# Second ConvFFN: seven products of quarters for 17 of its 22 pairs of up-projected tiles, their weight sums made beside the GLU

## The chip, the cores and the metric

The kernel runs on one core of a Trainium2 chip. Its time is the device time of one execution in microseconds (us), lower is better; the runs shown here are the median of three executions, 2302.68 us (2302.12 to 2303.56).

A core has TensorE (PE, matrix products into PSUM), VectorE (DVE), ScalarE (ACT), GpSimd (POOL) and SyncE (SP), each with a queue of instructions that it runs in order, and 16 DMA engines that all queues share. A DMA is issued by an instruction on SP's, ACT's or POOL's queue.

## The reference, cut to what matters

One step of a two-layer streaming encoder over T = 1088 tokens of width 1024 (1024 of a prompt, 64 of a sample). Layer 0 is windowed attention and a ConvFFN, layer 1 a state-space mixer that ends in a GLU (`y = (a + b_a) * sigmoid(b + b_b)`, where a and b are two products of the mixer's output with 1024 x 1024 weights) and a second ConvFFN. The change touches that GLU and the second ConvFFN:

```
u  = rms_norm(x, g6) @ w_up          # 1024 -> 2 x 2816: 22 gate tiles and 22 value tiles of 128 rows
u  = depthwise causal conv of width 3 over tokens (a bias and three taps per row)
gd = gelu(u[gate]) * u[value]        # 2816 rows
x  = x + rms_norm(gd @ w_down, g7)   # 2816 -> 1024
```

## The kernel before, in words

Rows of features lie on the 128 partitions, tokens along the free dimension. Tokens go in three blocks of 384, 384 and 320 (`BLK`). Every product of weights and activations is made of three passes over a high and a low part of both operands (`mm3`, L201 to L204: low activation, high activation, high activation by low weight), so that one 128 x 1024 weight tile against one block is 8 slices x 3 = 24 matmuls. ACT makes the high part of a weight tile and DVE the low part (L196, L197: `whl<-raw`); weight tiles are loaded in the order of a list (`wsrc`), two ahead of use, and six `big` buffers hold them.

**GLU** (L1204 to L1233). 24 tiles (8 rows of tiles x 3 blocks). Each has two PSUM tiles, `pb` and `pa`, of 24 matmuls; then ACT makes `sg` from `pb` (L1225) and DVE makes `y` from `pa` and `sg` (L1226). `sg` is one of five buffers (`t4`) that in the feed-forward hold the tiles `u` and `t`. `tile_` is a generator of two steps, the last 6 matmuls and the two instructions behind them being the second.

**Up-projection** (`up`, `up_start`, `up_block`, L359 to L392). For each of the 44 tiles: 3 blocks x 24 matmuls of a weight tile with the normalised input `h` (`hh`, `hl` in the trace), whose scale per token, `rb`, is multiplied in when DVE moves PSUM to `u` (L373, L375).

**Conv and gate** (`conv`, `gate`, L377 to L402). ACT makes the first tap (L381), DVE the other two (L382, L383), ACT the gelu (L396), DVE the product of gate and value in two pieces (L399, L401), which go to DRAM (`gd`) by SP's queue.

**Sums for the down-projection** (`sums_w`, `sums_g`, `sums`, L324 to L357). The down-projection of blocks 0 and 1 is done by seven products of quarters (`PRODUCTS`), which need sums of quarters of its weights (`jw`, written to `sd`) and of `gd` (`jg`, written to `td`). In the first ConvFFN the instructions are DVE's and the DMAs SP's (tiles `jt`); in the second both are POOL's (`E, Q`). Each of the 44 half-pairs has a turn (`aside`) in which one such job is started and the one before it is finished.

**What sets the order.** The program is written in this order, and a list scheduler with a priority per instruction (the order in which the program names them) lays each engine's queue; `order(x, y)` puts x behind y on the same engine.

Of the kernel before, what the change touches and what calls it, by code (L numbers as in the profile page):

```python
# [26 lines left out]
SIDE = 32  # L27

KCUT = (0, 12, 22)
GT = [[(4, "blkA")] * 3, [(4, "blkB"), (4, "blkB"), (2, "big")]]  # L30
# [11 lines left out]
class Core:  # L42
    def __init__(self, ctx, tc, a):
        self.ctx, self.tc, self.nc, self.a = ctx, tc, tc.nc, a
        nc = self.nc
        pool = lambda n, **k: ctx.enter_context(tc.tile_pool(name=n, bufs=1, **k))
        self.ready, self.wsrc = [], [("w_qk", 8), ("w_qk", 0), ("w_qk", 1), ("w_v", 0), ("w_v", 1)] + [("w_qk", m) for m in (2, 3, 9, 4, 5, 6, 7)]
        self.wsrc += [("w_o", m) for m in range(KD)]
        for i in range(2):
            self.wsrc += [("w_up", i, m + e) for m in range(KF) for e in (0, KF)]  # L50
            self.wsrc += [("w_part", i, k) + x[:3] for x in PRODUCTS for k in range(0, KH, 2)]
            self.wsrc += [("w_down", i, k, mh) for c in range(2) for mh in range(2) for k in range(KCUT[c], KCUT[c + 1], 2)]
            if i == 0:
# [113 lines left out]
    def load_unit(self, src):  # L167
        nc = self.nc
        raw = self.wts.tile([P, D], F32, name="raw", tag="raw", bufs=2)
        if src[0] == "w_part":  # L170
# [12 lines left out]
            nc.vector.tensor_sub(w[:, 1], raw, w[:, 0].bitcast(F32))  # L183
            return w
        ap = self.a[src[0]]
        if src[0] == "w_down":
# [4 lines left out]
        else:  # L191
            for i in src[1:]:
                ap = ap[i]
            self.loaded = nc.sync.dma_start(raw, ap)
        w = self.big([P, 2, D], "whl")
        nc.scalar.activation(w[:, 0], raw, AF.Copy)  # L196
# [112 lines left out]

    def ffn(self, i, h, rb, after, side=None, beside=lambda: None):  # L310

# [8 lines left out]


        E, Q = ((nc.vector, nc.sync), (nc.gpsimd, nc.gpsimd))[i]

        def sums_w(k):  # L324
            x = (jt[:, :2048] if i == 0 else js.tile([P, 2048], F32, name="jw")).rearrange("p (c h m) -> p c h m", c=2, h=2)
            Q.dma_start(x, a["w_down"][i, k::KH].rearrange("c p (h m) -> p c h m", h=2))
# [8 lines left out]
        def sums_g(k):  # L335
            x = jt[:, k % 2 * 1536:k % 2 * 1536 + 1536] if i == 0 else js.tile([P, 1536], F32, name="jg", bufs=2)
            x = x.rearrange("p (c b t) -> p c b t", c=2, b=2)
# [7 lines left out]
            Q.dma_start(td[:, k], x)  # L345

        jobs = {}

        def sums(j):

            for x in jobs.pop(j, []):
                next(x, None)
            k = (j // 2 - KH - 1, j // 2 - 2 * i)[j % 2]
            if 0 <= k < KH:
                x = (sums_g, sums_w)[j % 2](k)
                next(x)
                jobs[j + 1] = [x]  # L357

        def up_start(m):  # L359
            w = self.unit(("w_up", i, m))  # L360
# [4 lines left out]
            return w, u  # L365

        def up_block(w, u, b):
            t0, n = BLK[b]
            ps = self.mm_ps()
            for k in range(KD):  # L370
                self.mm3(ps[:, :n], w, slice(k * P, (k + 1) * P), h[b][0][:, k], h[b][1][:, k], k == 0, k == KD - 1)
            np_ = min(n, SEQ - t0)
            nc.vector.tensor_mul(u[:, t0 + 2:t0 + 2 + np_], rb[:, t0:t0 + np_], ps[:, :np_])  # L373
            if np_ < n:
                nc.vector.tensor_mul(u[:, SEQ + 4:], rb[:, SEQ:], ps[:, np_:n])  # L375

        def conv(m, u):  # L377
# [4 lines left out]
            nc.vector.scalar_tensor_tensor(t, u[:, 1:T + 3], cw(1, m), t, op0=ALU.mult, op1=ALU.add)  # L382
            nc.vector.scalar_tensor_tensor(t, u[:, 2:T + 4], cw(2, m), t, op0=ALU.mult, op1=ALU.add)  # L383
            return t
# [9 lines left out]
        def gate(f, us):  # L394
# [3 lines left out]
            tb = conv(KF + f, us.pop(KF + f) if KF + f in us else up([KF + f])[KF + f])  # L398
            nc.vector.tensor_mul(ta[:, :SEQ], ta[:, :SEQ], tb[:, :SEQ])  # L399
            nc.sync.dma_start(gd[:, f, :SEQ], ta[:, :SEQ])  # L400
            nc.vector.tensor_mul(ta[:, SEQ + 2:], ta[:, SEQ + 2:], tb[:, SEQ + 2:])  # L401
            nc.sync.dma_start(gd[:, f, SEQ:], ta[:, SEQ + 2:])  # L402

        turns = iter(range(2 * KF))

        def aside():
# [5 lines left out]
            sums(j - 1)  # L412

        us = up([0, KF, 1])
        gate(0, us)
        if i == 0:
            jt = self.yp.tile([P, 3072], F32, name="jt", tag="ypA", bufs=2)
        else:
            js_ctx = tc.tile_pool(name="js", bufs=1)
            js = js_ctx.__enter__()  # L420
        aside()
        for f in range(1, KF):
            if f == KF - 2:
                us = up([f, KF + f, f + 1])
# [4 lines left out]
        if i == 1:  # L429
            js_ctx.__exit__(None, None, None)  # L430
        nc.gpsimd.dma_start(a["o_conv"][i], cst.rearrange("p m s j -> p (m s j)"))
# [8 lines left out]
        def operand(p):  # L440
# [625 lines left out]
    def ssm(self, after):  # L1066
# [234 lines left out]
def build(tc, a):  # L1301
    nc = tc.nc
    with ExitStack() as ctx:
# [27 lines left out]
        def then(post, xs, xo, pre):  # L1331
# [61 lines left out]
```

## Time and profile before

| | |
|---|---|
| median of three runs | 2302.68 us |
| the profiled execution, its own time | 2296.63 us |
| its span | 2294.8 us |
| mean granted TensorE clock over the span | 0.986 |
| busy in the span: PE, DVE, ACT, POOL | 97%, 67%, 42%, 20% |
| GLU, its matmuls | 1315 to 1513 us |
| second up-projection, its matmuls | 1513 to 2039 us |
| second down-projection and the end | 2039 to 2295 us |

The profile is of one execution that took 6 us less than the median. An engine's busy time is the time in which an instruction of it runs. A matmul of 384 columns is shown as 0.33 to 0.35 us long but the next starts 0.17 us after it, since they overlap: the pace of PE is read from starts. "A <- B" in the columns on idle time and waits means that A's instruction began when B's had ended.

### The profile page before, as it was taken

To read this page: it belongs to the slowest core of one execution; us is meant where nothing else is said; L and a number is where in the kernel's file an instruction comes from. 1 tells how busy PE (TensorE), PEld (TensorE's weight loads), DVE (VectorE), ACT (ScalarE), POOL (GpSimd) and SP (SyncE) were. 2 spreads that over 40 slices of the span, in tenths; PEclk is the share of its full clock that TensorE was granted. 3 is DMA by queue.
4 is the path that set the end of the run, shared out by engine and by line. 5 is a ranking of instruction groups with operands and counts; after the bars stand their busy time and mean duration, and the time that the engine had idled before them with its cause. 6 is when DMAs were issued, how large, how long until landed. Compare 5 with 4: busy or idle time off the path is not lost.

```text
span 2294.8 us, 35768 instructions
## 1 busy us (share of the span) xinstructions
PE 2217.1 (97%) x13995; PEld 2149.1 (94%) x13995; DVE 1545.3 (67%) x2740; ACT 955.5 (42%) x1743; POOL 462.4 (20%) x416
## 2 busy tenths in 40 slices
PE   8999999999999999999978899999999999999997
PEld 7987799999999999999966699999999999999997
DVE  8677648989877786767757821397665555466764
ACT  5256756422343332555545631353222222245543
POOL 5222005100224223001100000154442132221000
PEclk9999999999999999999988999999999999999999
DMA  5100015655345655877759731155553333358773
GB/s 193 36 27 22 19 61 180 230 194 199 113 135 182 200 174 175 280 269 237 241 189 301 230 99 37 37 180 193 183 211 129 120 135 134 135 176 297 227 255 100
DMA packets 191001, 374.98 MB, mean 163 GB/s; under 512 B 23952, under 2 KB 114864, under 8 KB 187888
## 3 DMA queue, kind: packets, MB, share of 16 engines
q1 hardware_dynamic: 172736, 320.99, 42.1%
q0 software_dynamic: 9776, 47.21, 5.8%
q10 hardware_dynamic: 8320, 4.49, 0.9%
q8 instruction: 110, 1.80, 0.3%
q14 instruction: 59, 0.48, 0.1%
HBM read 262.10 MB, written 110.54 MB: 162 GB/s over the span
## 4 chain that ended last, share of the span: by engine, by line
PE 50%; DVE 6%; DMA 6%; ACT 3%; issue 2%; POOL 1%; SPq 1%; ACTq 0%; DVEq 0%; POOLq 0%
PE mm L202 14%; PE mm L204 14%; PE mm L203 14%; DMA raw<-sd 1%; PE pb L202 1%; PE pb L204 1%; PE pb L203 1%; PE pa L202 1%; PE pa L203 1%; PE pa L204 1%; DMA raw<-in_w_down 1%; DMA yd<-ys 1%; DMA prm<-b 1%; DMA prm<-oc 1%; DVE whl L197 1%
## 5 line engine op out<-in xcount | busy, mean ns | idle before, releaser
L202 PE MATMUL mm<-hl,whl 128*128 128x384 f32 (+1 forms) x2232 | 736.4, 330 | 11.0 <-ACT whl L196 7.4
L204 PE MATMUL mm<-hh,whl 128*128 128x384 f32 (+1 forms) x2232 | 734.3, 329 | 1.9 <-DVE whl L197 1.9
L203 PE MATMUL mm<-hh,whl 128*128 128x384 f32 (+1 forms) x2232 | 735.8, 330 | 0.0
L202 PEld LDWEIGHTS mm<-hl,whl 128*128 128x128 f32 x2232 | 420.8, 189 | 12.7 <-ACT whl L196 7.4
L204 PEld LDWEIGHTS mm<-hh,whl 128*128 128x128 f32 x2232 | 420.8, 189 | 2.7 <-DVE whl L197 2.7
L203 PEld LDWEIGHTS mm<-hh,whl 128*128 128x128 f32 x2232 | 421.1, 189 | 0.1
L196 ACT ACTIVATE whl<-raw 128x1024 fp32r<-128x1024 f32 x168 | 176.8, 1057 | 415.1 <-PE mm L204 330.2
L202 PE MATMUL mm<-gt,whl 128*128 128x384 f32 (+1 forms) x968 | 317.9, 329 | 2.3 <-ACT whl L196 1.8
L204 PE MATMUL mm<-gt,whl 128*128 128x384 f32 (+1 forms) x968 | 316.7, 328 | 0.7 <-DVE whl L197 0.7
L203 PE MATMUL mm<-gt,whl 128*128 128x384 f32 (+1 forms) x968 | 316.8, 328 | 0.0
L197 DVE TENSOR_TENSOR whl<-raw,whl 128x1024 fp32r<-128x1024 f32 x168 | 216.1, 1290 | 95.9 <-ACT whl L196 95.7
L373 DVE TENSOR_TENSOR u<-rb,mm 128x384 f32<-128x384 f32 (+1 forms) x264 | 131.7, 506 | 184.5 <-PE mm L204 184.3
L202 PEld LDWEIGHTS mm<-gt,whl 128*128 128x128 f32 x968 | 182.5, 189 | 3.2 <-ACT whl L196 2.0
L204 PEld LDWEIGHTS mm<-gt,whl 128*128 128x128 f32 x968 | 182.4, 189 | 1.0 <-DVE whl L197 1.0
L203 PEld LDWEIGHTS mm<-gt,whl 128*128 128x128 f32 x968 | 182.5, 189 | 0.0
L182 ACT ACTIVATE whl<-raw 128x1024 fp32r<-128x1024 f32 x84 | 82.8, 986 | 154.9 <-PE mm L204 60.9
L183 DVE TENSOR_TENSOR whl<-raw,whl 128x1024 fp32r<-128x1024 f32 x84 | 95.7, 1144 | 75.2 <-ACT whl L182 74.4
L383 DVE SCALAR_TENSOR_TENSOR t<-u,ppt,t 128x1090 f32<-128x1090 f32 x88 | 137.8, 1565 | 1.5
L382 DVE SCALAR_TENSOR_TENSOR t<-u,ppt,t 128x1090 f32<-128x1090 f32 x88 | 131.3, 1492 | 9.8 <-ACT t L381 7.4
L301 POOL TENSOR_TENSOR y<-y,xl 128x768 f32<-128x768 f32 (+1 forms) x16 | 30.3, 1892 | 491.5 <-DVE y L298 397.8
L381 ACT ACTIVATE t<-u,ppt 128x1090 f32<-128x1090 f32 x88 | 114.3, 1299 | 12.9 <-DVE t L383 6.8
L396 ACT ACTIVATE t<-t 128x1090 f32<-128x1090 f32 x44 | 49.1, 1117 | 132.7 <-DVE t L383 132.5
(345 smaller groups left out, 3690.0 us busy)
## 6 DMA issues: line engine op xcount, KB each, us to landing
raw<-in_w_up SPq DMA_DIRECT2D x88, 512.0 KB, 3.9
raw<-in_w_down SPq DMA_DIRECT2D x74, 512.0 KB, 4.4
gd<-t SPq DMA_DIRECT2D x44, 512.0 KB, 3.0
raw<-sd SPq DMA_DIRECT2D x40, 512.0 KB, 4.5
pm<-prm SPq DMA_DIRECT2D x32, 522.0 KB, 7.1
gr<-td SPq DMA_DIRECT2D x40, 384.0 KB, 6.1
jt<-in_w_down SPq DMA_DIRECT2D x11, 1024.0 KB, 5.8
sd<-jt SPq DMA_DIRECT2D x11, 1024.0 KB, 4.0
```

Of the source, the lines that this page charges most:

```text
L182: nc.scalar.activation(w[:, 0], raw, AF.Copy)
L183: nc.vector.tensor_sub(w[:, 1], raw, w[:, 0].bitcast(F32))
L196: nc.scalar.activation(w[:, 0], raw, AF.Copy)
L197: nc.vector.tensor_sub(w[:, 1], raw, w[:, 0].bitcast(F32))
L202: nc.tensor.matmul(out, w[:, 0, sl], xl, start=start, stop=False)
L203: nc.tensor.matmul(out, w[:, 0, sl], xh, start=False, stop=False)
L204: self.last_mm = nc.tensor.matmul(out, w[:, 1, sl], xh, start=False, stop=stop)
L373: nc.vector.tensor_mul(u[:, t0 + 2:t0 + 2 + np_], rb[:, t0:t0 + np_], ps[:, :np_])
L381: nc.scalar.activation(t, u[:, 0:T + 2], AF.Identity, bias=cb(m), scale=cw(0, m))
L382: nc.vector.scalar_tensor_tensor(t, u[:, 1:T + 3], cw(1, m), t, op0=ALU.mult, op1=ALU.add)
L383: nc.vector.scalar_tensor_tensor(t, u[:, 2:T + 4], cw(2, m), t, op0=ALU.mult, op1=ALU.add)
L396: nc.scalar.activation(ta, ta, AF.Gelu_apprx_tanh)
```

## The change

In the second ConvFFN the pairs f = 5 to 21 (`PLAIN = 5`) make their two tiles for blocks 0 and 1 by seven products of quarters (`seven`): the quarters are gate and value row tiles (two), the halves of the 1024 input rows (two), and blocks 0 and 1 (two). Each product is 4 slices x 3 passes = 12 matmuls of 384 columns. Block 2 is computed as before.

What goes with it:

- Sums of the weights' quarters (`su` in DRAM; two halves for each of 17 pairs, 34 jobs) are made in the GLU: `sums(f, e)` there loads two pieces of 256 KB on POOL's queue into a `t4` tile `sj`, makes four DVE operations of 128 x 256, and stores 512 KB on POOL's queue. `beside()` starts one after each of the GLU's 48 half steps until all are started, and finishes the one of two half steps before.
- In the ConvFFN each of the 17 pairs loads two weight units more (`w_sum`, 512 KB, split on ACT and DVE as the others are).
- The seven products need the normalised activations and sums of them. `ys`, the residual stream's tiles that the norm left in SBUF, are multiplied in place with scale and gain on DVE (`normed`: 16 operations of 128 x 384 at f = 2, 8 of 128 x 320 at f = 4), summed (`input_sums`: 8 of 128 x 768 at f = 3), and split into high and low parts on ACT and DVE over `h`'s own tiles and two of `yp` (`into_place`: six of 128 x 1536 at f = 4, one at f = 3, two of 128 x 1280 at f = 5). `rb` is then in the operands, not in the move from PSUM.
- For a pair by seven products DVE moves PSUM to `u` by seven additions of 128 x 384 (one product goes by ACT's copy, one stays in PSUM for an addition); block 2 is moved by ACT from the pair f = 6 on.
- `sums_w` and `sums_g` of the second ConvFFN are DVE's, with DMAs on POOL's queue, and `sums_w` starts six pairs later. `gd` of the second ConvFFN is stored by POOL's queue. Gate times value is one operation over 1090 columns, in both ConvFFNs. The tiles that pair 20 of the second ConvFFN took ahead (`up([f, KF + f, f + 1])`) are left to the first.

The core of the diff:

```diff
+PLAIN = 5
@@ the list of weight units
-            self.wsrc += [("w_up", i, m + e) for m in range(KF) for e in (0, KF)]
+            for m in range(KF):
+                sums = [("w_sum", m, e) for e in range(2)] if i == 1 and m >= PLAIN else []
+                self.wsrc += [("w_up", i, m)] + sums + [("w_up", i, m + KF)]
@@ ffn
-        E, Q = ((nc.vector, nc.sync), (nc.gpsimd, nc.gpsimd))[i]
+        E, Q = nc.vector, (nc.sync, nc.gpsimd)[i]
...
+            if normed:
+                nc.scalar.activation(u[:, t0 + 2:t0 + 2 + np_], ps[:, :np_], AF.Copy)
+                nc.scalar.activation(u[:, SEQ + 4:], ps[:, np_:n], AF.Copy)
+                return
...
-            nc.vector.tensor_mul(ta[:, :SEQ], ta[:, :SEQ], tb[:, :SEQ])
-            nc.sync.dma_start(gd[:, f, :SEQ], ta[:, :SEQ])
-            nc.vector.tensor_mul(ta[:, SEQ + 2:], ta[:, SEQ + 2:], tb[:, SEQ + 2:])
-            nc.sync.dma_start(gd[:, f, SEQ:], ta[:, SEQ + 2:])
+            nc.vector.tensor_mul(ta, ta, tb)
+            Q.dma_start(gd[:, f, :SEQ], ta[:, :SEQ])
+            Q.dma_start(gd[:, f, SEQ:], ta[:, SEQ + 2:])
...
+        def input_sums():
+            b11, b21, b12, b22 = (half(x[b], j) for b in range(2) for j in range(2))
+            t1, t4 = (self.big([P, 4, 384], "t", F32) for _ in range(2))
+            t2 = ts.tile([P, 4, 384], F32, name="t2", tag="t2")
+            for o, u, v in ((t1, b12, b11), (b12, b22, b12), (t2, b22, t1), (t4, b21, t2)):
+                for k in (slice(0, 2), slice(2, 4)):
+                    self.order(V.tensor_sub(o[:, k], u[:, k], v[:, k]), self.last_conv)
...
+        def seven(f, first):
...
+            nc.scalar.activation(g1, product(w, 0, "b11"), AF.Copy)
+            V.tensor_add(g0, g1, product(w, 1, "b21"))
+            ws = self.unit(("w_sum", f, 0))
+            V.tensor_add(g1, g1, product(ws, 0, "t2", True))
+            p3 = product(ws, 1, "b22", True)
+            if not first:
+                up_block(w, ug, 2, True)
+            ws = self.unit(("w_sum", f, 1))
+            V.tensor_add(v1, g1, product(ws, 0, "t3", True))
+            V.tensor_add(g1, g1, p3)
+            p5 = product(ws, 1, "t1", True)
+            V.tensor_add(g1, g1, p5)
+            w = self.unit(("w_up", i, KF + f))
+            V.tensor_add(v0, v1, product(w, 1, "t4"))
+            V.tensor_add(v1, v1, p5)
+            up_block(w, uv, 2, not first)
...
         for f in range(1, KF):
-            if f == KF - 2:
+            if i == 1 and f == 2:
+                normed((0, 1))
+            if i == 1 and f == 3:
+                late = input_sums()
+            if i == 1 and f == PLAIN - 1:
+                us = up([f, KF + f])
+                into_place(*late)
+                normed((2,))
+            if i == 1 and f >= PLAIN:
+                us = seven(f, f == PLAIN)
...
@@ ssm, the GLU
+        def sums(f, e):
+            x = self.t4([P, 2, 2, 256], "sj")
+            for j in range(2):
+                nc.gpsimd.dma_start(x[:, j], a["w_up"][1, j * KF + f].rearrange("p (c q) -> p c q", c=2)[:, :, 256 * e:256 * e + 256])
+            yield
...
+            V.tensor_add(a22, a21, a22)
+            V.tensor_sub(a21, a11, a21)
+            V.tensor_sub(a11, a22, a11)
+            V.tensor_sub(a12, a12, a11)
+            nc.gpsimd.dma_start(su[f, e], x.rearrange("p j c q -> p j (c q)"))
...
             for x in order[:3] * 2 + [x for x in order[3:] for _ in range(2)]:
                 next(x)
+                beside()
```

Three places of the queues show what moves. The first is DVE's queue in the pairs 2 to 4 of the second ConvFFN, before the change: only conv, gate, PSUM moves and weight splits stand there.

```order
L382 SCALAR_TENSOR_TENSOR t<-u,ppt,t 128x1090
L373 TENSOR_TENSOR u<-rb,mm 128x256
L375 TENSOR_TENSOR u<-rb,mm 128x64
L197 TENSOR_TENSOR whl<-raw,whl 128x1024
L383 SCALAR_TENSOR_TENSOR t<-u,ppt,t 128x1090
L399 TENSOR_TENSOR t<-t 128x1024
```

After the change (L402 is the second conv tap, L392 and L394 the PSUM moves, L418 the gate product, L208 the weight split; L456 are the sums of the input, L438 the splits):

```order
L402 SCALAR_TENSOR_TENSOR t<-u,ppt,t 128x1090
L456 TENSOR_TENSOR t<-y 128x768 x2
L418 TENSOR_TENSOR t<-t 128x1090
L456 TENSOR_TENSOR y<-y 128x768
L456 TENSOR_TENSOR t_15202<-y,t 128x768
L392 TENSOR_TENSOR u<-rb,mm 128x256
L394 TENSOR_TENSOR u<-rb,mm 128x64
L456 TENSOR_TENSOR y<-y 128x768
L456 TENSOR_TENSOR t_15202<-y,t 128x768
L438 TENSOR_TENSOR t_15212<-t,t_15211 128x1536
L456 TENSOR_TENSOR t<-y,t_15202 128x768
L374 MEMSET u 128x2
```

Right behind these rows stand the last PSUM move of block 0 and the weight splits of pair 4: the eight sums and the first split have moved ahead of them.

The second place is the same queue in a pair by seven products at which both kinds of sums for the down-projection run (f from 12 to 16; L489 to L502 are the additions out of PSUM, L339 to L342 the sums of `jw`, L351 to L354 those of `jg`):

```order
L342 TENSOR_TENSOR jw<-jw 128x512
L353 TENSOR_TENSOR jg<-jg 128x384
L491 TENSOR_TENSOR u<-u,mm 128x384
L418 TENSOR_TENSOR t<-t 128x1090
L208 TENSOR_TENSOR whl<-raw,whl 128x1024
L354 TENSOR_TENSOR jg<-jg 128x384
L208 TENSOR_TENSOR whl<-raw,whl 128x1024
L496 TENSOR_TENSOR u<-u,mm 128x384
L497 TENSOR_TENSOR u<-u,mm 128x384
L499 TENSOR_TENSOR u<-u,mm 128x384
L501 TENSOR_TENSOR u<-u,mm 128x384
```

In the program before, the operations on `jw` and `jg` stand on POOL's queue, each job between its own load and store, as here for `jw`:

```order
L326 DMA jw<-in_w_down 128x2x1024
L329 TENSOR_TENSOR jw<-jw 128x512
L330 TENSOR_TENSOR jw<-jw 128x512
L331 TENSOR_TENSOR jw<-jw 128x512
L332 TENSOR_TENSOR jw<-jw 128x512
L333 DMA sd_14364<-jw 128x2048
```

A pair's share of DVE's queue has grown by these eight sums, two weight splits (four instead of two) and one addition out of PSUM, less the moves of block 2, which ACT has now.

The third place is POOL's queue at the GLU. Before, the store of the mixer's state is followed at once by the norm behind the GLU:

```order
L1204 DMA out_o_st<-fo 128x128
L301 TENSOR_TENSOR y<-y,xl 128x768
L273 TENSOR_SCALAR gx<-y,ppt 128x384
L301 TENSOR_TENSOR y<-y,xl 128x768
L274 TENSOR_TENSOR hl<-gx,hh 128x384
```

After, 102 DMAs stand between the two (`L312` is the norm's addition now). They begin so:

```order
L1310 DMA out_o_st<-fo 128x128
L1319 DMA sj<-in_w_up 128x2x256 x6
L1327 DMA su<-sj 128x1024 x2
L1319 DMA sj<-in_w_up 128x2x256 x2
L1327 DMA su<-sj 128x1024
```

They end so:

```order
L1319 DMA sj<-in_w_up 128x2x256 x4
L1327 DMA su<-sj 128x1024
L1319 DMA sj<-in_w_up 128x2x256 x2
L1327 DMA su<-sj 128x1024 x3
L312 TENSOR_TENSOR y<-y,xl 128x768
```

Each store (L1327) waits for DVE's four sums, and the loads behind it in the queue start only once it is issued.

## Rows read from the trace of the kernel before

**Rows 1.** The profile page, part 1: busy us of each engine, share, instructions.

```profile
PE 2217.1 (97%) x13995; PEld 2149.1 (94%) x13995; DVE 1545.3 (67%) x2740; ACT 955.5 (42%) x1743; POOL 462.4 (20%) x416
```

**Rows 2.** Busy us by stretch: PE, PEld, DVE, ACT, POOL, clock, DMA share, GB/s.

```profile
1340.00:1476.00 136.00, 136.00 (x814) 136.00 (x814) 30.67 (x50) 34.91 (x51) 0.00 (x0) 1.00 0.13 39
1560.00:1608.00 48.00, 48.00 (x293) 48.00 (x292) 41.69 (x53) 19.93 (x28) 22.92 (x16) 1.00 0.54 196
1608.00:2039.00 431.00, 431.00 (x2616) 431.00 (x2615) 241.64 (x328) 109.47 (x165) 124.07 (x103) 1.00 0.41 145
...
440.00:600.00 160.00, 159.86 (x966) 159.86 (x967) 144.76 (x421) 47.01 (x69) 0.00 (x0) 1.00 0.51 181
```

**Rows 3.** Waits of PE, 1512 to 2039 us: us in total, times, longest.

```profile
PE mm L202 <- POOL hl L274: 0.4, 1, 0.4
```

**Rows 4.** Timeline of PE in the second up-projection: start us, duration us.

```profile
1799.69 0.31 PE L204 MATMUL mm<-hh,whl 128*128 128x320 f32 x1
...
1801.59 0.34 PE L202 MATMUL mm<-hl,whl 128*128 128x384 f32 x1
...
1802.13 0.34 PE L202 MATMUL mm<-hl,whl 128*128 128x384 f32 x1
...
1804.22 0.33 PE L202 MATMUL mm<-hl,whl 128*128 128x384 f32 x1
```

**Rows 5.** DVE by line and shape, first up-projection, 400 to 570 us.

```profile
L382 DVE SCALAR_TENSOR_TENSOR t<-u,ppt,t 128x1090 f32<-128x1090 f32 x15 | 20.3, 1351 | 0.2
...
L197 DVE TENSOR_TENSOR whl<-raw,whl 128x1024 fp32r<-128x1024 f32 x15 | 18.2, 1220 | 1.0 <-ACT whl L196 1.0
L373 DVE TENSOR_TENSOR u<-rb,mm 128x384 f32<-128x384 f32 x27 | 14.4, 550 | 0.4 <-PE mm L204 0.4
...
L330 DVE TENSOR_TENSOR jt<-jt 128x512 f32<-128x512 f32 x10 | 7.0, 697 | 0.0
```

**Rows 6.** DVE by line and shape, second up-projection, 1560 to 2039 us.

```profile
L383 DVE SCALAR_TENSOR_TENSOR t<-u,ppt,t 128x1090 f32<-128x1090 f32 x42 | 67.6, 1608 | 1.3
...
L438 DVE TENSOR_TENSOR gt<-gr,gt 128x768 fp32r<-128x768 f32 x4 | 3.6, 954 | 0.1
```

**Rows 7.** Second conv tap, 1560 to 2039 us: duration ns min/median/max, first and last start.

```profile
L383 DVE SCALAR_TENSOR_TENSOR t<-u,ppt,t x42: 1348/1356/2382, 1564.5 to 2030.8; 128x1090 f32<-128x1090 f32 x42
```

**Rows 8.** ACT by line and shape, second up-projection, 1560 to 2039 us.

```profile
L381 ACT ACTIVATE t<-u,ppt 128x1090 f32<-128x1090 f32 x43 | 55.8, 1298 | 8.8 <-DVE t L383 6.8 <-DMA gd<-t 2.0
L196 ACT ACTIVATE whl<-raw 128x1024 fp32r<-128x1024 f32 x35 | 37.1, 1060 | 228.9 <-PE mm L204 228.9
L396 ACT ACTIVATE t<-t 128x1090 f32<-128x1090 f32 x21 | 23.5, 1118 | 59.8 <-DVE t L383 59.8
```

**Rows 9.** GLU, 1340 to 1513 us, by line and shape.

```profile
L1226 DVE SCALAR_TENSOR_TENSOR y<-pa,ppt,sg 128x384 f32<-128x384 f32 x16 | 9.8, 616 | 69.4 <-ACT sg L1225 69.4
```

**Rows 10.** POOL's DMA issues, 1512 to 2039 us: busy us, mean ns.

```profile
L326 POOL DMA_DIRECT2D jw<-in_w_down x11 | 7.8, 711 | 45.7 <-DMA sd<-jw 43.3 <-PE mm L204 2.4
...
L333 POOL DMA_DIRECT2D sd<-jw x11 | 6.3, 577 | 3.3 <-POOL jw L332 3.3
```

**Rows 11.** DMA issues, 1512 to 2039 us: KB each, median us to landing.

```profile
jw<-in_w_down POOLq DMA_DIRECT2D x11, 1024.0 KB, 5.7
sd<-jw POOLq DMA_DIRECT2D x11, 1024.0 KB, 4.4
gd<-t SPq DMA_DIRECT2D x21, 512.0 KB, 2.7
...
raw<-in_w_down SPq DMA_DIRECT2D x1, 256.0 KB, 2.5
```

**Rows 12.** Busy us by stretch behind a wait of PE in the first up-projection.

```profile
782.10:785.50 3.40, 3.40 (x12) 3.40 (x11) 2.25 (x3) 1.60 (x4) 3.32 (x2) 0.51 0.95 311
785.50:790.00 4.50, 4.50 (x27) 4.50 (x27) 2.46 (x3) 0.00 (x0) 4.36 (x4) 1.00 0.47 135
```

**Rows 13.** Waits of PE, 570 to 930 us: us in total, times, longest.

```profile
PE wps L948 <- DVE kt L942: 9.1, 4, 3.4
```

More of the change, by code (lines that the diff above doesn't have):

```diff
@@ L306, in post_norm, with ffn @@
         return apply
-    def ffn(self, i, h, rb, after, side=None, beside=lambda: None):
+    def ffn(self, i, h, rb, after, side=None, beside=lambda: None, x=None, g=None):
         nc, tc, a = self.nc, self.tc, self.a
@@ L345, in sums_g @@
             Q.dma_start(td[:, k], x)
+        w0 = (PLAIN + 1) * i
+        starts = {2 * (k + w0) + 1: sums_w(k) for k in range(KH)}
+        starts.update({2 * (k + KH) + 2: sums_g(k) for k in range(KH)})
         jobs = {}
@@ L412, in aside, with half, split, normed @@
             sums(j - 1)
+        def half(v, j):
+            return v[:, 4 * j:4 * j + 4]
+        def split(hi, lo, src):
+            nc.scalar.activation(hi, src, AF.Copy)
+            nc.vector.tensor_sub(lo, src, hi.bitcast(F32))
+        def normed(bs):
+            for b in bs:
+                t0, n = BLK[b]
+                for k in range(KD):
+                    v = nc.vector.scalar_tensor_tensor(x[b][:, k], x[b][:, k], g[:, k:k + 1], rb[:, t0:t0 + n], op0=ALU.mult, op1=ALU.mult)
+                    self.order(v, self.last_conv)
@@ new lines, in input_sums @@
+        def input_sums():
+            V = nc.vector
+            b11, b21, b12, b22 = (half(x[b], j) for b in range(2) for j in range(2))
[4 more added lines that the diff above has]
+                    self.order(V.tensor_sub(o[:, k], u[:, k], v[:, k]), self.last_conv)
+            op["t1"] = [ts.tile([P, 4, 384], F32R, name=f"t1{j}") for j in range(2)]
+            split(*op["t1"], t1)
+            return t2, t4
@@ new lines, in into_place @@
+        def into_place(t2, t4):
+            todo = [("b11", 0, 0), ("b21", 0, 1), ("t2", t2), ("b22", 1, 1), ("t3", 1, 0), ("t4", t4)]
+            for name, src, *j in todo:
+                if j:
+                    hi, lo = (half(v, j[0]) for v in h[src][:2])
+                    src = half(x[src], j[0])
+                else:
+                    y = self.yp.tile([P, 2, 4, 384], F32R, name="th", tag="ypA", bufs=2)
+                    hi, lo = y[:, 0], y[:, 1]
+                op[name] = hi, lo
+                split(hi, lo, src)
@@ new lines, in seven, with product @@
+        def seven(f, first):
+            V = nc.vector
+            ug, uv = u_tile(f), u_tile(KF + f)
+            g0, g1, v0, v1 = (u[:, 2 + 384 * j:386 + 384 * j] for u in (ug, uv) for j in range(2))
+            def product(w, j, o, sums=False):
+                ps = self.mm_ps()[:, :384]
+                for k in range(4):
+                    c = (k // 2 * 4 + 2 * j + k % 2 if sums else 4 * j + k) * P
+                    self.mm3(ps, w, slice(c, c + P), op[o][0][:, k], op[o][1][:, k], k == 0, k == 3)
+                return ps
+            w = self.unit(("w_up", i, f))
+            if first:
+                up_block(w, ug, 2)
+            nc.scalar.activation(g1, product(w, 0, "b11"), AF.Copy)
[14 more added lines that the diff above has]
+            up_block(w, uv, 2, not first)
+            return {f: ug, KF + f: uv}
@@ L418, in ffn @@
         else:
-            js_ctx = tc.tile_pool(name="js", bufs=1)
-            js = js_ctx.__enter__()
+            ts_ctx = tc.tile_pool(name="ts", bufs=1)
+            ts = ts_ctx.__enter__()
+            op = {}
         aside()
         for f in range(1, KF):
-            if f == KF - 2:
+            if i == 1 and f == 2:
[8 more added lines that the diff above has]
+                us = seven(f, f == PLAIN)
+                if f == PLAIN:
+                    for j in range(2):
+                        split(half(h[2][0], j), half(h[2][1], j), half(x[2], j))
+            if i == 0 and f == KF - 2:
                 us = up([f, KF + f, f + 1])
@@ L1206, in ssm, with beside @@
         ws = {}
+        su = self.su = self.dram.tile([KF, 2, P, 2, 512], F32, name="su")
+        def sums(f, e):
+            x = self.t4([P, 2, 2, 256], "sj")
+            for j in range(2):
+                nc.gpsimd.dma_start(x[:, j], a["w_up"][1, j * KF + f].rearrange("p (c q) -> p c q", c=2)[:, :, 256 * e:256 * e + 256])
+            yield
+            a11, a12, a21, a22 = x[:, 0, 0], x[:, 0, 1], x[:, 1, 0], x[:, 1, 1]
+            V = nc.vector
+            V.tensor_add(a22, a21, a22)
[3 more added lines that the diff above has]
+            nc.gpsimd.dma_start(su[f, e], x.rearrange("p j c q -> p j (c q)"))
+        jobs = iter([sums(f, e) for f in range(PLAIN, KF) for e in range(2)])
+        loaded = []
+        def beside():
+            loaded.append(next(jobs, iter(())))
+            next(loaded[-1], None)
+            if len(loaded) > 2:
+                next(loaded.pop(0), None)
         with self.boundary():
```

42 lines of the change are left out of this document (24 added, 18 removed).

## The prediction

> **What bounds the kernel now.** I read the page first: PE is busy 97% of the span and no other engine over 67% [rows 1]. Then the stretches: in the second up-projection PE is busy for 431.00 of 431 us, in the GLU for 136.00 of 136, both at a granted clock of 1.00, which is the higher level, 2.4 GHz [rows 2]. The view of waits finds 0.4 us of PE waiting for any engine from 1512 to 2039 us [rows 3]. So both places run at PE's own pace; a matmul less there is time less, and work added to another engine costs something only where PE comes to wait for it. The timeline gives the pace: 12 starts of 384 columns in 1804.22 − 1802.13 = 2.09 us, 0.174 us each; 13 of 320 columns in 1.90 us, 0.146 us each [rows 4]. A pair of tiles is 96 × 0.174 + 48 × 0.146 = 23.7 us now. Of that DVE is busy 241.64 / 431 = 56%, so 13.3 us, and ACT 25% [rows 2].
>
> **What goes.** A pair of quarter products has 7 × 12 = 84 matmuls of 384 columns instead of 96. In 17 pairs that is 204 matmuls fewer, 204 × 0.174 = **35.5 us**, and a pair of 84 × 0.174 + 7.0 = 21.6 us. The whole term is on the path, because nothing else ends a wait there. The pace of the new matmuls is taken as that of the old: operands of the same 128 x 128 and 128 x 384 form, weights still changed for each.
>
> The Trainium skill (TensorE: Matmul & The Clock Gate, section Back-to-back issue gap) gives the isolated gap of a matmul at the full clock as columns / 2.4 GHz plus 2.5 ns, an estimate of 162.5 ns for 384 columns. By it the term would be 33.2 us; the trace's 174 ns is longer and decides.
>
> **What DVE gets in a pair by seven products.** Durations come from the first up-projection, where DVE makes the same sums and POOL is idle [rows 2, 5]:
> - four weight splits of 1.22 us, 4.9 (two before);
> - four conv operations of 1.35, 5.4;
> - the gate product over 1090 columns, at most a conv's 1.35, taken as 1.3;
> - seven additions out of PSUM, as the multiplication out of PSUM of 0.55, 3.9.
>
> That is 15.5 us. The sums moved from POOL add 4 × 0.70 = 2.8 (pairs 6 to 16) and, as 384 columns from SBUF are taken at the same 0.55, 4 × 0.55 = 2.2 (pairs 12 to 21): 18.3, 20.5 and 17.7 us against PE's 21.6. In the five pairs 12 to 16 DVE is at 95%. What a DVE that full costs PE, the first up-projection shows: 144.76 of 160 us busy, 90%, and PE loses 0.14 us [rows 2]. A relief goes the other way: with POOL summing, the second conv tap takes 1608 ns on average and up to 2382, while its median is 1356 [rows 6, 7]; the 88 POOL operations leave, so the undisturbed durations are right for after. I take 0. Below nothing it can't go, since PE has no idle time to give back there; above, if every operation took 10% more, 22.5 us in the five pairs, 0.9 × 5 = 4.6. ACT gets four splits of 1.06, two taps of 1.30, a gelu of 1.12 [rows 8], a copy of 384 columns and two moves of block 2 (together at most three taps, 3.9): 11.9 us at most of 21.6, so it hides.
>
> **The hand-over, pairs 2 to 5.** DVE gets, once: 16 scalings at the GLU's 0.62 [rows 9], 9.9; eight sums of 768 at 0.95 [rows 6], 7.6; seven splits of 1536, which by the slope from 384 (0.55) to 768 (0.95) are 0.95 + 2 × 0.40 = 1.76, 12.3; eight scalings of 320 at about 0.55, 4.4; two splits of 1280 at about 1.5, 3.0. In all 37 us, in four pairs in which DVE has 4 × (23.7 − 13.3) = 42 us free. It fits on average but not in its order: in pair 3 the sums and the first split, 9.4 us, stand ahead of the weight splits of pair 4, and the product that reads `t1` waits for ACT's copy of the first product, which stands behind a gelu that waits for DVE. Two of the sums' tiles also take buffers of weight tiles. Going through the queue with each instruction as long as its row, I get PE waiting twice, 4 + 5 = 9 us; with the closest packing of the same queue 2 us in all. A wait has a price beyond itself: after the longest wait of PE for `kt`, 3.4 us [rows 13], the clock granted over the next 3.4 us was 0.51, the lower level of 1.2 GHz, and back at 1.00 after it [rows 12], so about 1.7 us lost; two such make 3.4. From 0 (if the queue's lag is all taken up) to 13 us; I take **6**, the middle, as neither walk is nearer to a row.
>
> **The GLU.** A tile of it is (2 × 48 × 0.174 + 48 × 0.146) / 3 = 7.9 us of PE. With 34 jobs in 34 of 48 half steps DVE gets 136 operations of 128 x 256, by the slope from 512 (0.70) and 384 (0.55) 0.40 each, 54 us in a stage where it is busy 30.67 of 136 [rows 2]; POOL, idle there, gets 68 load issues of about 0.71 and 34 stores of 0.58 [rows 10], 68 us of 190. The wait added is `sg`'s: it shares five buffers with `sj`, and a buffer comes free only when a job's store has landed. Behind a waiting `sg` stand DVE's `y`, which frees the PSUM tiles, and so PE two tiles later. I walked the five buffers through the 34 jobs with equal landing times for loads and stores: up to 7 us cost 0 to 10 us in all, 8 us 17 to 29, 9 us 48. The rows near to them are 2.5 us for 256 KB, 2.7 for 512 KB and 5.7 for 1 MB [rows 11]. Traffic speaks for more: 34 × 1.05 MB = 35.7 MB in 17 tiles, 134 us, are 266 GB/s on top of 39 [rows 2], and the trace has a stretch where 311 GB/s kept the DMA engines busy to 0.95 [rows 12]. Twice the small landings is still 5 to 5.5 us. From 0 to 10; I take **0**, as the nearest rows lie under 6.
>
> The loads ahead of `w_up` in the ConvFFN (34 × 512 KB in 370 us, 48 GB/s beside 145 at a DMA share of 0.41 [rows 2]) hide. The stores of `gd` on POOL's queue stand in line with waits for DVE's sums, but the first reader is the down-projection or a `jg` job two turns later. At the end, pair 21 delivers its gate a little later than now and the first product's loads find other buffers: 0 to 1 us, taken 0.5.
>
> **Sum.** −35.5 + 0 + 6 + 0 + 0.5 = −29. Against the profiled execution's 2296.63 us that is 2267.6; that execution lies 6 us under the median of the runs, and on the median, 2302.68, it is **2274 us**. With the terms' ends, −35.5 + 0 to −35.5 + 4.6 + 13 + 1, the forecast's own range is 2267 to 2286 (the GLU's 10 us are left to its rival).
>
> **The rivals.**
> - *DVE becomes the bound.* DVE runs in order, additions out of PSUM stand behind conv operations, and PE has a handful of PSUM tiles. If it is late by 0.8 us in each of the 17 pairs, 13.6 us go: with the hand-over 2274 + 14 = 2288. For it: 95% in five pairs, 82 to 85% in the rest. Against: PE gapless at 90%. Chance 0.17.
> - *The GLU is held by its buffers.* This is the one that ends slower. One mechanism: jobs keep `t4` buffers until their stores land, `sg` waits. It decides from landings of about 8.5 us: there the 29 us gained are lost, at 9 us the time is 2274 + 48 = 2322, at 8 us about 2291 to 2303. For it: 305 GB/s asked for, in small pieces on POOL's queue, in order behind waits for DVE; against: landings under 6 us in every row of POOL's queue [rows 11]. Chance 0.15, most of it net slower.
> - *The products are fewer but the gain isn't there*: groups of 12 matmuls instead of 24, with another PSUM tile and another operand each 2.1 us, at 0.18 us apiece would cost 17 × 84 × 0.006 = 9 us, 2283; or the hand-over takes double its upper end, 2294. Chance 0.06.
>
> In the GLU the issue itself may be what grows. In the trace POOL issued DMAs in 711 and 577 ns [rows 10], also in the stretch where DVE was busy 41.69 of 48 us [rows 2]. The Trainium skill (SBUF — State Buffer, section SBUF: two separate sides) warns that a DMA issued by GpSimd can't get its descriptors written while DVE runs in a mode that takes both shared ports, and gives 3100 ns in place of 620; at that, an estimate from the page, 102 issues would take 316 us, more than the whole GLU. The same page (section Who interferes with whom) says that a tensor-tensor operation has no such mode. DVE's work in the GLU is nearly all of that kind, and the issues above agree; so it adds a little to the second rival and nothing to the sum.
>
> **Chances.** Forecast 0.62, DVE bound 0.17, GLU held 0.15, gain not there 0.06. What a measurement of this kernel can tell from no change is 0.2%, 4.6 us. Faster by more: 0.62 + 0.17, 0.02 of the GLU and 0.04 of the last, 0.85; within: 0.04 of the GLU (landings of 8.5 us) and 0.01 of the last together with another, 0.05; slower: 0.09 of the GLU and 0.01, 0.10. The range for 8 in 10 is 2265 to 2298: below, the 35.5 us whole and 2 us of what rows don't show; above, the first rival with a part of the second, leaving out the GLU at 9 us.
>
> **What the profile after would show.** PE's matmuls 204 fewer and the up-projection some 490 to 500 us long, with PE's waits in it all within the first six pairs and under 10 us. If instead waits for DVE's additions or splits recur in pairs 12 to 16, the first rival is right. In the GLU, PE busy throughout and `sj`'s landings under 7 us; if PE waits for `y` there, the second is. DVE's conv operations at 1.35 us in the second ConvFFN; were they still at 1.6, POOL's sums were not what slowed them and DVE would be over PE's 21.6 us in the five pairs. The forecast is wrong if PE idles more than 20 us between 1315 and the end of the up-projection, or if the pace of 384 columns is not 0.174.

## The result, and the profile after

The changed kernel takes 2273.27 us, the median of four runs (2267.74 to 2278.56), against 2302.4 us for the kernel before on the same chip (four runs, 2297.65 to 2303.56). The ratio is 0.9877 with a 95% interval of 0.985 to 0.9904, so 22 to 35 us less. The forecast was 2274 us. The profiled execution took 2273.49 us, its span 2271.7 us, 23 us less than the profiled execution before, which lay 6 us under its median. One of the four executions of a later experiment, the sigmoid in `y`'s place, took 12139.55 us and stands apart from all others; its numbers below are of the other three.

The page's first part, as [rows 1]: PE 28.6 us less busy, DVE 141 us more.

```profile
PE 2188.5 (96%) x13791; PEld 2118.9 (93%) x13791; DVE 1686.1 (74%) x2982; ACT 1021.7 (45%) x1867; POOL 418.2 (18%) x474
```

13995 − 13791 = 204 matmuls are gone, as counted. The stretches that answer to [rows 2] (PE, PEld, DVE, ACT, POOL, clock, DMA share, GB/s), the first of the GLU, the others of the up-projection (1797 to 1906 us are about the pairs 12 to 16):

```profile
1340.00:1476.00 136.00, 133.42 (x789) 133.13 (x788) 80.17 (x179) 32.91 (x49) 62.67 (x96) 0.99 0.84 290
...
1515.00:1945.00 430.00, 429.59 (x2617) 429.05 (x2617) 355.57 (x488) 187.71 (x304) 64.63 (x86) 1.00 0.56 195
...
1797.00:1906.00 109.00, 109.00 (x665) 109.00 (x664) 93.21 (x127) 46.27 (x81) 16.80 (x28) 1.00 0.76 274
...
1640.00:2010.00 370.00, 366.69 (x2217) 366.05 (x2216) 297.08 (x395) 158.90 (x271) 43.74 (x74) 1.00 0.65 228
```

PE loses 0.4 us from 1515 to 1945 us, the hand-over included, and loses more in the GLU and at the end of the up-projection. The waits of PE from 1300 to 2060 us (us in total, times, longest):

```profile
PE mm L213 <- DVE u L501: 5.6, 2, 3.2
PE pr L247 <- issue: 2.6, 1, 2.6
PE p L1275 <- DVE wk L1259: 1.8, 1, 1.8
PE p L1270 <- ACT ys L1279: 1.6, 1, 1.6
PE pb L213 <- DVE zl L1305: 1.0, 1, 1.0
PE mm L213 <- POOL hl L285: 0.4, 1, 0.4
```

Before the change, over the same stretch:

```profile
PE p L1164 <- ACT ys L1173: 5.2, 2, 3.5
PE pb L202 <- DVE zl L1199: 1.2, 1, 1.2
PE mm L202 <- POOL hl L274: 0.4, 1, 0.4
```

A ledger of the two profiled executions, by PE's starts in the timeline, shows where the difference lies (us):

| stretch | before | after | difference |
|---|---|---|---|
| start to the first product of the GLU | 1315.29 | 1310.93 | −4.4 |
| GLU, first to last product | 197.05 | 203.03 | +6.0 |
| up-projection, to the first product behind it | 526.86 | 497.07 | −29.8 |
| from there to the end of the span | 255.64 | 260.68 | +5.0 |

The up-projection's −29.8 is the −35.5 of the forecast and 5.7 of loss, of which 4.8 are the wait shown next and the slower clock behind it. So the forecast's total came out near, but of its terms only the −35.5 is found in this ledger.

**The late waits.** This is PE, DVE and POOL around the longest one (start us, duration us; in brackets what the engine waited for):

```profile
1941.03 0.72 POOL L348 DMA_DIRECT2D jg<-gd  x1 [2.74 <-DMA gd<-t]
...
1947.59 0.56 DVE L351 TENSOR_TENSOR jg<-jg 128x384 f32<-128x384 f32 x1 [6.69 <-DMA jg<-gd]
1948.07 1.22 DVE L208 TENSOR_TENSOR whl<-raw,whl 128x1024 fp32r<-128x1024 f32 x1
1949.20 0.55 DVE L352 TENSOR_TENSOR jg<-jg 128x384 f32<-128x384 f32 x1
...
1949.67 0.55 DVE L501 TENSOR_TENSOR u<-u,mm 128x384 f32<-128x384 f32 x1
```

```profile
1946.72 0.34 PE L215 MATMUL mm<-th,whl 128*128 128x384 f32 x1
1950.27 0.69 PE L213 MATMUL mm<-hl,whl 128*128 128x384 f32 x1 [3.21 <-DVE u L501]
1950.76 0.52 PE L214 MATMUL mm<-hh,whl 128*128 128x384 f32 x1
1951.08 0.52 PE L215 MATMUL mm<-hh,whl 128*128 128x384 f32 x1
...
1953.58 0.33 PE L214 MATMUL mm<-hh,whl 128*128 128x384 f32 x1
1953.76 0.33 PE L215 MATMUL mm<-hh,whl 128*128 128x384 f32 x1
```

POOL issues the load of `jg` only when a store of `gd` has landed (1941.03). DVE reaches the first sum of it and stands for 6.69 us while what stands behind it has to wait, since its queue is in order: the addition L501, which frees a PSUM tile, is three instructions behind. PE stops for 3.21 us, and up to 1953.3 us its matmuls start 0.32 us apart instead of 0.17: the granted clock is 0.50 there, the lower of the two levels (1.2 GHz). A second such wait, 2.4 us, stands at the first products of the down-projection. PE is in pair 19 at the first of them and past pair 21 at the second, later than DVE's fullest pairs, 12 to 16.

**The GLU.** Landing of `sj`'s DMAs (min/median/max), and what ended the idle time ahead of `sg`, 1340 to 1476 us (us, times):

```profile
DMA to landing us min/median/max: 2.9/5.9/9.3
```

```profile
  DMA su<-sj: 46.5, 8
  DVE y L1357: 16.0, 3
```

Eight of the 18 `sg` waited for a job's store. PE, which runs ahead by the PSUM tiles that are free, lost time to it once: the norm behind the last tile of block 0 was late, and its product `pr` waited 2.6 us, with some 1.6 us lost to the lower clock behind it. The rest of the GLU's 6.0 is a lower clock (0.50) over its first 4.3 us, behind waits of PE at the mixer's end; the kernel of the first experiment, which has no jobs, starts its GLU at a lower clock too, so this part is not shown to come from the change.

### The profile page after: what moved, and what is told of

Read it like the earlier page. It is cut to its first block, busy times and chain, and to the rows that moved or that the text cites. A ratio compares the mean times of both kernels' runs of the same rounds, so it can differ in the third digit from the quotient of the medians.

```text
span 2271.7 us, 35981 instructions
## 1 busy us (share of the span) xinstructions
PE 2188.5 (96%) x13791; PEld 2118.9 (93%) x13791; DVE 1686.1 (74%) x2982; ACT 1021.7 (45%) x1867; POOL 418.2 (18%) x474
## 5 line engine op out<-in xcount | busy, mean ns | idle before, releaser
L213 PE MATMUL mm<-hl,whl 128*128 128x384 f32 (+1 forms) x1960 | 645.2, 329 | 14.6 <-ACT whl L207 7.7
L215 PE MATMUL mm<-hh,whl 128*128 128x384 f32 (+1 forms) x1960 | 642.3, 328 | 1.8 <-DVE whl L208 1.8
L214 PE MATMUL mm<-hh,whl 128*128 128x384 f32 (+1 forms) x1960 | 643.9, 329 | 0.0
L213 PEld LDWEIGHTS mm<-hl,whl 128*128 128x128 f32 x1960 | 369.8, 189 | 16.8 <-ACT whl L207 7.7
L207 ACT ACTIVATE whl<-raw 128x1024 fp32r<-128x1024 f32 x202 | 212.7, 1058 | 355.6 <-PE mm L215 167.4
L215 PEld LDWEIGHTS mm<-hh,whl 128*128 128x128 f32 x1960 | 369.6, 189 | 2.6 <-DVE whl L208 2.6
L214 PEld LDWEIGHTS mm<-hh,whl 128*128 128x128 f32 x1960 | 370.0, 189 | 0.0
L208 DVE TENSOR_TENSOR whl<-raw,whl 128x1024 fp32r<-128x1024 f32 x202 | 252.5, 1255 | 101.2 <-ACT whl L207 100.8
L187 DVE TENSOR_TENSOR whl<-raw,whl 128x1024 fp32r<-128x1024 f32 x84 | 94.8, 1133 | 71.7 <-ACT whl L186 71.4
L186 ACT ACTIVATE whl<-raw 128x1024 fp32r<-128x1024 f32 x84 | 82.8, 987 | 125.2 <-DMA raw<-sd 48.7
L401 DVE SCALAR_TENSOR_TENSOR t<-u,ppt,t 128x1090 f32<-128x1090 f32 x88 | 123.3, 1403 | 9.4 <-ACT t L400 8.8
L402 DVE SCALAR_TENSOR_TENSOR t<-u,ppt,t 128x1090 f32<-128x1090 f32 x88 | 123.2, 1401 | 0.4
L392 DVE TENSOR_TENSOR u<-rb,mm 128x384 f32<-128x384 f32 (+1 forms) x164 | 80.2, 501 | 23.3 <-PE mm L215 18.4
L312 POOL TENSOR_TENSOR y<-y,xl 128x768 f32<-128x768 f32 (+1 forms) x16 | 31.4, 1961 | 349.0 <-DVE y L309 284.3
L544 DVE TENSOR_TENSOR gt<-gr,gt 128x768 fp32r<-128x768 f32 (+2 forms) x106 | 90.1, 879 | 4.3 <-ACT gt L543 3.6
```

Of the source, the lines that this page charges most:

```text
L213: nc.tensor.matmul(out, w[:, 0, sl], xl, start=start, stop=False)
L214: nc.tensor.matmul(out, w[:, 0, sl], xh, start=False, stop=False)
L215: self.last_mm = nc.tensor.matmul(out, w[:, 1, sl], xh, start=False, stop=stop)
L402: self.last_conv = nc.vector.scalar_tensor_tensor(t, u[:, 2:T + 4], cw(2, m), t, op0=ALU.mult, op1=ALU.add)
L544: nc.vector.tensor_sub(x[:, 1, u], raw, x[:, 0, u].bitcast(F32))
```

## The experiments

Theory A, from these rows: the gain is the 204 matmuls; what is given back comes from DVE standing at `jg` (about 9 us) and from `sg` waiting for stores (about 4 us). The rivals are a DVE that is simply full, and differences between executions: the mixer's stretch, from its first product to the GLU's, is 103 to 110 us long in ten profiled executions that share its code. So times are compared by medians of several executions, and places by their waits. The first four experiments ran on one chip and the last four on another; each ratio is to the kernel before on the same chip.

**No quarter products.**

```diff
-PLAIN = 5
+PLAIN = 22
```

and the hand-over left out with it.

> The changed kernel with all 22 pairs of the second ConvFFN by plain products: no quarter products, no weight sums in the GLU, no hand-over; what stays is the rest of the change (sums for the down-projection on DVE, their DMAs and gd's stores on POOL's queue, one gate product). Theory A (the gain is the 204 matmuls, and what is given back comes from the quarter products' company): 2302 us, within 3 us of the kernel before, no wait of PE over 1 us between 1515 and 2040 us. Rival (DVE waiting for jg at the head of its queue costs PE by itself): two waits of PE behind DVE at the end of the up-projection and about 2311 us.

Measured 2296.59 us, ratio 0.9981 (0.9969 to 0.9994). The up-projection is 528.6 us long, before 526.9, with one wait for DVE, of 1.5 us, where none over 1 us was expected. So the quarter products carry the gain; the sums of `jg` on DVE cost PE no wait at the end where DVE has time over. But a time 1 to 7 us under the kernel before was in no theory, and it went before the GLU: the down-projection of the first ConvFFN starts at 933.0 us instead of 939.1.

**Sums of `jg` finished a turn later.**

```diff
-                jobs[j + 1] = [x]
+                jobs.setdefault(j + 1 + i * (1 - j % 2), []).append(x)
```

> The changed kernel with the sums of jg in the second ConvFFN finished two turns after their load is issued instead of one. Theory A (PE's two waits late in the up-projection, 3.4 and 2.6 us with about 1.5 us of lower clock behind each, come from DVE standing at a jg sum whose load has not landed, with the additions out of PSUM queued behind): both waits go, PE waits under 1 us between 1640 and 2040 us, about 9 us less, 2264. Rival (DVE is simply full in these pairs): the same work, waits of the same size elsewhere, 2273. Second rival: the last td lands later and the down-projection waits for it: waits of PE behind 2020 us, 2270 to 2275.

Measured 2275.52 us, ratio 0.9891 (0.9872 to 0.991). The edit was empty (the two waits that the expectation gives as 3.4 and 2.6 us are the 3.2 and 2.4 of the view): the scheduler laid the same queues on DVE and POOL, instruction for instruction. It is a second sample of the changed kernel: the same kind of waits at `jg` (3.7, 0.7 and 2.4 us), and early in the GLU a wait for `zl` of 4.5 us where the first sample had 1.0, with 0.4 for `pr`.

**The sigmoid in `y`'s place.**

```diff
-                sg = self.t4([P, n], "sg")
+                sg = y[b][:, m]
```

> The changed kernel with the GLU's sigmoid written into y's own place instead of a t4 buffer, so that it no longer waits for a job's store to land. Theory A (PE's wait of 2.7 us at 1470 us and the lower clock behind it come from the shared buffers: sg waits for the stores of su): the wait goes, 4 us less, 2269, and sg waits for nothing but PE. Rival (DVE, in order, stands at sj sums whose loads land late, and y is queued behind them): y stays as late, the wait at 1470 stays, 2273.

Measured 2267.89 us, ratio 0.987 (0.9849 to 0.989): not told apart from the changed kernel by time. The wait of PE in the GLU, from 1325 to 1515 us, shows the edit working and something else:

```profile
PE pb L213 <- DVE zl L1305: 4.5, 1, 4.5
```

The wait for `pr` at 1470 us is gone; the one for `zl`, some 25 us into the GLU, where the mixer's last part comes in, is the whole of what is left. The same edit with the empty one (2270.75 us, ratio 0.9878, 0.986 to 0.9897) was meant as the two together and is a repeat of this:

> Both edits: the sigmoid in y's place and the sums of jg finished a turn later. Theory A: the two savings add, 2273 - 9 - 4 = 2260 us, and PE waits under 2 us in all from 1320 us to the end of the up-projection. Rivals as for the two edits: 2264 if only the later sums help, 2269 if only the sigmoid does, 2273 if neither.

It has no wait at 1470 either, and 3.8 us for `zl`.

**The first ConvFFN's gate product, alone in the kernel before.**

```diff
-            nc.vector.tensor_mul(ta[:, :SEQ], ta[:, :SEQ], tb[:, :SEQ])
+            if i == 0:
+                nc.vector.tensor_mul(ta, ta, tb)
+            else:
+                nc.vector.tensor_mul(ta[:, :SEQ], ta[:, :SEQ], tb[:, :SEQ])
...
-            nc.vector.tensor_mul(ta[:, SEQ + 2:], ta[:, SEQ + 2:], tb[:, SEQ + 2:])
+            if i == 1:
+                nc.vector.tensor_mul(ta[:, SEQ + 2:], ta[:, SEQ + 2:], tb[:, SEQ + 2:])
```

> The kernel before with one edit alone: in the first ConvFFN the product of gate and value is one DVE operation instead of two. Theory B (the rest of the change gains about 4 us ahead of the GLU, because DVE is the late engine of the first ConvFFN, where PE's transposes wait for kt): 4 to 5 us less, 2295, and PE waits for kt under 6 us instead of 9.1. Rival (the 4 us are a difference between executions): 2299, and waits for kt of 9 us.

Measured 2291.31 us, ratio 0.9962 (0.995 to 0.9975), 6 to 12 us less. DVE's share of it is small: two operations of 1356 and 218 ns became one of 1448. But DVE is what PE waits for there. Before, PE's waits from 570 to 935 us were the 9.1 us for `kt` [rows 13] and

```profile
PE wps L948 <- DVE u L362: 1.9, 1, 1.9
```

and now they are

```profile
PE wps L952 <- DVE kt L946: 4.0, 3, 2.2
PE wps L952 <- DVE w L766: 2.2, 2, 1.3
```

and the down-projection of the first ConvFFN starts at 933.9 us, as in every kernel with this edit (932.5 to 934.4 in nine). Why so small a share of DVE's work is worth that much is not shown beyond these waits.

**Sums of `jg` held behind the last addition of the next pair.**

```diff
+            self.last_add = V.tensor_add(v1, v1, p5)
...
+            s = E.tensor_sub(a11, a12, a11)
+            if i == 1:
+                self.order(s, self.last_add)
```

> The changed kernel with the first sum of each jg held behind the last addition out of PSUM of the next pair on DVE's queue; finishing the sums a turn later in the program had left the queue as it was. Theory A (PE's waits at the end of the up-projection and at the start of the down-projection come from DVE standing at a jg sum whose load has not landed): PE's waits for the additions go, under 1 us from 1640 us to the start of the down-projection, and 8 us are gained, 2264. Rival (DVE is full): waits as large, 2272. Second rival: td is later, and the down-projection waits for it instead, 2270.

Measured 2267.12 us, ratio 0.985 (0.9832 to 0.9869), 0.3 to 0.4% under the two samples of the changed kernel (its interval overlaps the first sample's and lies below the second's). The stretch of the late waits:

```profile
1640.00:2009.00 369.00, 369.00 (x2247) 369.00 (x2246) 302.90 (x402) 163.21 (x275) 44.51 (x75) 1.00 0.66 232
```

and DVE's waits for `jg`, in the changed kernel from 1640 to 2010 us and then with the edit in the stretch above (us in total, times, longest):

```profile
DVE jg L351 <- DMA jg<-gd: 26.6, 5, 6.7
...
DVE jg L351 <- DMA jg<-gd: 7.9, 2, 5.0
```

PE is gapless with DVE as busy as before the edit (302.90 of 369 against 297.08 of 370). The sums are the same, only later in the queue; so it was the standing ahead of the additions, not the work. DVE still stands for 7.9 us, and PE loses nothing by it. The next stretch, to the span's end, is 257.5 us long instead of 260.7: the wait at the down-projection's start is gone too, and PE waits for no `td`. How much the standing costs differs between executions: the up-projection is 491.8 us long with this edit, and 497.1, 498.8, 493.2, 496.7 and 492.5 in the five kernels with quarter products and without it.

**The first loads of `sj` behind the mixer's last transfer**, with the sigmoid in `y`'s place:

```diff
-                nc.gpsimd.dma_start(x[:, j], ...)
+                v = (nc.sync if 2 * f + e < 2 * PLAIN + 3 else nc.gpsimd).dma_start(x[:, j], ...)
+                if 2 * f + e < 2 * PLAIN + 3:
+                    self.order(v, self.last_yf)
```

> The changed kernel with the GLU's sigmoid in y's place, and the loads of the first three jobs on SP's queue behind the mixer's last transfer (yf), so that they can't run beside it. Theory C (the early loads of sj delay the mixer's last transfers and with them the first tile of the GLU, by 1 to 5 us): PE's wait for zl at the start of the GLU goes under 1 us, 3 to 4 us less than with the sigmoid alone, 2267, and the GLU is 199 us long or less. Rival (the wait for zl differs between executions whatever is loaded; before it was 1.4 us): a wait of 1 to 5 us, 2271.

Measured 2263.63 us, ratio 0.9835 (0.9819 to 0.985), about 8 to 10 us under the two samples of the sigmoid alone (0.987 and 0.9878; its interval touches the first's and lies below the second's); the GLU is 195.6 us long and PE waits for nothing in it. How the transfers collided is seen on ACT and POOL in the changed kernel (first fence) and with the edit of `jg`, which leaves the GLU's program as it is (second): the mixer's last part goes out to DRAM as `yd` and comes back as `yf`.

```profile
1320.35 1.44 POOL L1319 DMA_DIRECT2D sj<-in_w_up  x2 [4.94 <-ACT z L1298]
1321.62 0.37 ACTq L1282 DMA_DIRECT2D yd<-ys  x1
...
1333.57 2.15 ACT L1295 ACTIVATE z<-yf 128x1024 f32<-128x1024 f32 x1 [11.02 <-DMA yf<-yd]
```

```profile
1318.54 0.37 ACTq L1284 DMA_DIRECT2D yd<-ys  x1
...
1333.69 2.02 ACT L1297 ACTIVATE z<-yf 128x1024 f32<-128x1024 f32 x1 [14.23 <-DMA yf<-yd]
```

From the issue of `yd` to `z` it takes 12.0 and 15.2 us here, and 15.6, 15.6 and 15.0 in the three other executions with early loads; without them 9.9 (no quarter products), 12.2 (the kernel before), 12.0, 10.7 and 10.6 (with all edits). PE's wait for `zl` was 1.0, 4.5, 4.5, 3.8 and 4.0 us with early loads and 0, 0, 0, 1.1 and 1.2 without (1.2 is the kernel before, for which the expectation has 1.4), and the GLU 202.2 to 209.2 us long against 195.5 to 197.1. So the early loads delay the mixer's last part in four of the five; in the profiled execution of the changed kernel itself they did not: its 12.0 and 1.0 us are those of a kernel without them.

**All three.**

> All three edits: jg's sums behind the last addition, the sigmoid in y's place, the first loads of sj behind yf. If theories A and C hold the savings add: 2271 - 8 - 3 = 2260 us, PE waits under 3 us in all from the start of the GLU to the start of the down-projection. If only one holds, 2264 or 2267.

Measured 2255.64 us (2253.82 to 2258.93), ratio 0.9808 (0.9795 to 0.9822): faster than both kernels, and the lowest of all runs here. The GLU and the up-projection:

```profile
1308.00:1503.00 195.00, 195.00 (x1205) 194.56 (x1205) 119.70 (x258) 67.22 (x109) 79.70 (x106) 1.00 0.76 258
1503.00:1995.00 492.00, 492.00 (x2998) 491.69 (x2997) 410.28 (x560) 219.06 (x354) 69.95 (x99) 1.00 0.57 199
```

The expectation was 2260; PE has no wait from the GLU to the down-projection. From the GLU's last product to the first behind the up-projection it is 491.29 us: 35.57 less than before, and 204 x 0.174 is 35.5.

## Why the prediction was right, and where it was not

- **What goes, −35.5:** right in mechanism and size. With all waits away the up-projection is 35.57 us shorter. The pace of 384 columns stayed at 0.174 us with groups of 12.
- **DVE in a pair, 0:** the durations were right: the second conv tap went from 1608 ns on average [rows 6] to 1348 once POOL made no sums (without quarter products, from 1560 to 2005 us, 1353; with the gate product alone, POOL still summing, 1649), and the additions took 0.55 us (DVE by line and shape, 1640 to 2010 us):

```profile
L402 DVE SCALAR_TENSOR_TENSOR t<-u,ppt,t 128x1090 f32<-128x1090 f32 x34 | 45.7, 1348 | 0.1
...
L489 DVE TENSOR_TENSOR u<-u,mm 128x384 f32<-128x384 f32 x17 | 9.3, 547 | 0.0
```

DVE is busy 80% of that stretch, and 93.21 of 109 us, 86%, in the pairs for which the prediction had 95%; PE loses nothing there, so the first rival's full DVE is not what cost time. The step that failed is the one on the transfers behind the moved sums: "the first reader is the down-projection or a `jg` job two turns later". The load of that job waits for the stores of `gd`, and its sum stood at the head of DVE's queue before the load had landed; in the profiled execution that is most of the 5.7 us lost in the up-projection and of the 5.0 behind it (5.3 and 3.2 less with the sums held back). The sign given for it failed too: PE's waits were to lie within the first six pairs, and came at the end. The prediction asked what DVE costs when full and not what it costs when it stands; the first rival named the right place (waits for additions out of PSUM) with the wrong cause, and in other pairs than it said.
- **The hand-over, 6:** wrong, it was 0. PE waits 0.4 us from 1550 to 1945 us, for `hl`, as before the change. The nearer of the two walks was the one with the closest packing, 2 us: DVE's operations start closer than their durations, as these rows show, where two sums of 0.95 take 1.82 together and the next starts 1.74 after the first.

```profile
1599.62 1.82 DVE L456 TENSOR_TENSOR t<-y 128x768 f32<-128x768 f32 x2
1601.36 1.28 DVE L418 TENSOR_TENSOR t<-t 128x1090 f32<-128x1090 f32 x1
1602.57 0.95 DVE L456 TENSOR_TENSOR y<-y 128x768 f32<-128x768 f32 x1
```

- **The GLU, 0 taken, 0 to 10 given:** 6.0 us, inside the bounds. The wait of `sg` for stores is the second rival's mechanism, at landings of 5.9 us median, about twice the rows of before, as bounded; it reached PE once and cost about 4.2 of the 6.0. The collision of the first loads with the mixer's last transfers was not thought of: the queues that a new transfer runs beside were weighed in the stages of the change, not at the edge before it. It cost nothing in this execution; in four others PE's wait was 3.8 to 4.5 us, where 0 to 1.2 is seen without early loads. POOL's 68 load issues took 718 ns in the median, 711 before, with DVE busy 59% of 1340 to 1476 us, mostly with tensor-tensor operations. The Trainium skill describes a lock-out of GpSimd's descriptors by DVE's two-port modes (SBUF — State Buffer, section SBUF: two separate sides), and says that a tensor-tensor operation has no such mode (section Who interferes with whom); the 718 ns agree.
- **Left out:** the gate product in one piece changes the first ConvFFN too, and the sum has no term for that. It is worth about 5 us in the traces (939.1 to 933.4) and 6 to 12 by the ratio. [rows 13] held the reason: PE waited for DVE there.
- **The end, 0.5:** not shown. Of the 5.0 above 3.2 go with the edit of `jg`; what is left, 257.5 us against 255.64, is as long in the kernels without quarter products (257.5 and 257.0).

Measured terms: −4.4 + 6.0 − 29.8 + 5.0 = −23.2 between the profiled executions, where −29 was forecast; between the medians it is −29.1, since the profiled execution before was a quick one, and by the two samples (0.9877, 0.9891) about 27 us. That the forecast lay within 1 us of the median is luck in part: 4.4 us of gain that it missed and 6.5 us that it gave away for the hand-over and the end stood against 17 us of losses that its sum took at nothing.

It stays open whether moving the sums of the second ConvFFN to DVE costs or gains by itself: without quarter products 0.9981, with the gate product alone 0.9962, with intervals that overlap, and profiled spans of 2292.4 and 2291.8 us.

## What to carry to other kernels

An engine with an in-order queue has two prices: its work, and the time in which it stands at an instruction whose data have not landed; only the first shows in its busy share. When a job with a transfer is moved to such an engine, place it behind the instructions that the critical engine waits for, with a dependency if a scheduler orders the queue, and look at the queue to see that the edit moved anything. Standing alone is no cost: DVE stood 50.4 us at the sums of `sj` in the GLU and 26.6 at those of `jg`, and PE lost time only where an instruction that it waited for was queued behind. Read a diff for every caller of the edited function, and the transfers of a new stage against the last transfers of the stage before.

## What the runs showed of the hardware

The length of a wait of PE did not decide alone whether the granted clock fell. Waits of 2.4 us at the same place, the start of the down-projection, were followed by a clock of 0.50 in the changed kernel and in its second sample, and by 1.00 in the kernels with the sigmoid in `y`'s place and with the loads held back. In the up-projection a wait of 1.95 us was followed by 0.50 (the repeat of the sigmoid), one of 1.5 us was not. At 0.50 the matmuls of 384 columns ran at 0.32 us a step, the level of 1.2 GHz, for about ten of them, some 1.6 us lost each time.

At 290 GB/s over 136 us, a DMA share of 0.84, loads of 256 KB landed in 5.9 us in the median, where one took 2.5 in a stretch at 145 GB/s [rows 11]. With all three edits those on POOL's queue took 6.5 us in the median, and PE waited for nothing in the GLU.
